# The sample tile's latents in float32 on four column groups, and an earlier page table load, in the first stage of a decode step

## The chip, the cores and the metric

The kernel runs on one core of one Trainium2 chip. The metric is the device time of one execution in microseconds; the time before is the median of three runs. The profile is of one further execution of the same program on the same kind of core.

## The reference, cut to what matters

One step of a hybrid decoder over 1024 prompt rows and 32 sample rows (8 sequences of 4 tokens). The part that the change touches is the norm of the input and the projection to the MLA latents:

```python
def rmsnorm(x, w):
    xf = x.astype(jnp.float32)
    xf = xf * lax.rsqrt(jnp.mean(xf * xf, axis=-1, keepdims=True) + EPS)
    return xf.astype(x.dtype) * w

z = rmsnorm(x, ln_w) @ w_in              # D_MODEL = 1024
rq, rk, rv, rg, cq, ckv, kr, mg, ga, gb = split(z)
q = rmsnorm(cq, q_norm_w) @ w_uq         # cq: 384 columns
ckv = rmsnorm(ckv, kv_norm_w)            # ckv: 256 columns
kr = rope(kr, pos)                       # kr: 64 columns
```

The 384 + 256 + 64 = 704 columns are called the latents. The sample rows then attend to a paged cache, for which `page_table` (8 x 64 numbers) is turned into a list of rows to gather. All results are float32, and the products are wanted at about that precision.

## The kernel before

The 1056 rows stand in nine tiles: tiles 0 to 7 are the prompt (128 rows each), tile 8 is the sample (32 rows). Most products are made in a split form: a float32 operand is parted into a rounded high part and a low remainder (both of type float32r), and `mac` (L261) adds three matmuls, high by high, high by low and low by high. The kernel is written in a framework that places the semaphores and lays out the order of each engine's instructions itself, by priority (the order of the source) and by its own estimate of when operands are ready. The order in a trace is therefore not line by line that of the source.

The first stage does this:

- `load_x(t)` (L300) loads a tile of x. `turn_tile(t)` (L342) squares and sums it on ACT (into a scratch tile `xs`, two buffers), makes the reciprocal root on POOL (`rstd_of`, L229), transposes the tile on PE in eight 128-column pieces (`turn_input`, L313), copies them out of PSUM and stores them to `xTD`.
- `scale_tile(t)` (L351) spreads the reciprocal root over the partitions with a small matmul (L355), multiplies on DVE (`y`, L358), and writes the high parts (`xh`, ACT, L363) and the low ones (`xl`, DVE, L364), eight of each. They stay in SBUF as `xn` for all later products of this input.
- `load_lat(k)` (L305) loads rows 128k to 128k+127 of the latents' weights into a raw tile `wlr` (four buffers for eight loads), makes the high part on ACT or POOL in turn, and the low part on DVE (`lo_of`, L198). A raw buffer is free again when both are made.
- `latent_tile(t)` (L386) makes the latents of a tile: 8 x 3 matmuls of 384 columns into one PSUM bank and 8 x 3 of 320 into another, with the tile's rows as the stationary operand; then the two norms (ACT L398, POOL, DVE L400), the rotation (`rope_nat`, L367) and the stores. For tile 8 the stationary operand has 32 columns, the number of matmuls is the same 48, and the result is kept in `latS`.
- `page_rows()` (L427) loads the page table, spread over all partitions, and turns it into the row numbers `idx` with four DVE instructions (L431 to L436). Its two tiles `pt_all` and `own` share the two `xs` buffers.

The tiles go in the order 0, 1, 8, 2, 3, 4, 5, 6, 7 (L444). Before the loop over them, tile 0 is turned and scaled, the weights are loaded, with x tiles 1 and 8 among them, and tile 1 is turned and scaled. In the loop `latents()` (L456), step n turns the tile two places on, makes the latents of its own tile, and scales the tile two places on. The page table follows in step 4. From step 6 the loop hands out time, and `beside` (L128) puts gate products (`gate_tiles`, L410) between: these load their weights into the two `wr` buffers of the pool `wst` and store their results through the two `gev` buffers of the same pool. All DMAs named here are issued by SP, whose queue is in order: an issue that waits for a buffer holds those behind it.

A later part, `sample_queries` (L503), already has products of the form that the change uses: four float32 matmuls with 32 stationary columns each, written to the four 32-partition groups of one PSUM bank (L527). L655 and L686 are of that kind too.

Of the kernel before, what the change touches and what calls it, by code (L numbers as in the profile page):

```python
# [161 lines left out]
def decode_step(ctx: ExitStack, tc: tile.TileContext, A: dict, O: dict):  # L162
# [20 lines left out]
    def ac():  # L183
        return banks["pool"].tile([P, 512], F32, tag="ac", name="ac", bufs=3)
# [119 lines left out]

    def load_lat(k):  # L305
        hi, lo = (p1.tile([P, NLAT], F32R, tag=f"wl{s}{k}", name=f"wl{s}{k}", bufs=1) for s in "hl")
        raw = p1.tile([P, NLAT], F32, tag="wlr", name="wlr", bufs=4)
        sp.dma_start(raw, w_in[k * P:(k + 1) * P, C_LAT:C_LAT + NLAT])
        (hi_pool if k % 2 else act.copy)(hi, raw)
        lo_of(lo, raw, hi)  # L310
        wlat.append((hi, lo))

    def turn_input(t, src, dst, nf, by=act.copy):  # L313

# [27 lines left out]
    def turn_tile(t):  # L342
        n = rows(t)
        xt = xts.pop(t)
        ss = small(p1, "ss")
        xs = p1.tile([P, D], F32, tag="xs", name="xs", bufs=2)
        act.activation(xs[:n], xt[:n], AF.Square, accum_out=ss[:n])
        r = rstd_of(p1, ss, n, 1.0 / D, dve if t == 0 else pool)
        turned[t] = r, turn_input(t, xt, xTD, D // P, dve.tensor_copy if t == 0 else act.copy)

    def scale_tile(t):  # L351
# [31 lines left out]
    latS = lp.tile([NR, NLAT], F32, name="latS")  # L383
    idx = lp.tile([P, NB * NPG // 16], I32, name="idx")

    def latent_tile(t):  # L386
        n = rows(t)
        pq, pk = ac(), ac()
        for ps, lo, w in ((pq, 0, QL), (pk, QL, KL + ROPE)):
            for k in range(8):  # L390
                xk = tuple(v[:, t * P:t * P + n] for v in xn[k])
                wk = tuple(v[:, lo:lo + w] for v in wlat[k])
                mac(ps[:n, :w], xk, wk, k == 0, k == 7)
        la = latS if t == 8 else p1.tile([P, NLAT], F32, tag="la", name="la", bufs=2)
        cq, kv, kr = la[:n, 0:QL], la[:n, QL:QL + KL], la[:n, QL + KL:NLAT].unsqueeze(1)
        for src, dst, w, nw in ((pq[:n, :QL], cq, QL, qnw), (pk[:n, :KL], kv, KL, kvw)):
            ss = small(p1, "ss2")
            act.activation(dst, src, AF.Square, accum_out=ss[:n])  # L398
            r = rstd_of(p1, ss, n, 1.0 / w)
            dve.scalar_tensor_tensor(out=dst, in0=src, scalar=r[:n], in1=nw[:n], op0=ALU.mult, op1=ALU.mult)  # L400
        rope_nat(kr, pk[:n, KL:KL + ROPE].unsqueeze(1), t, n, p1, 1, "kro")
        if t < 8:
            sp.dma_start(O["ckv_prompt"][0, 0, t * P:(t + 1) * P, :], kv)
            sp.dma_start(O["krope_prompt"][0, 0, t * P:(t + 1) * P, :], la[:, QL + KL:])
            turn_blocks(latD, p1.tile([P, NLAT], F32, tag="lt", name="lt", bufs=2), la, t, P)
        else:
            sp.dma_start(O["ckv_sample"].rearrange("l b t c -> (l b t) c"), kv)
            sp.dma_start(O["krope_sample"].rearrange("l b t c -> (l b t) c"), la[:n, QL + KL:])
# [16 lines left out]
                 gate_tiles(C_RG, [t[:, f, :] for t in gtD for f in range(4)], range(16), AF.Silu), gate_tiles(C_MG, mgD, range(4), AF.Silu))  # L425

    def page_rows():  # L427
        pt_all = p1.tile([P, NB * NPG], I32, tag="xs", name="pt_all", bufs=2)
        sp.dma_start(pt_all, A["page_table"].rearrange("b n -> (b n)").unsqueeze(0).to_broadcast([P, NB * NPG]))
        own = p1.tile([P, NB * NPG], F32, tag="xs", name="own", bufs=2)  # L430
        dve.tensor_copy(own, pt_all)  # L431
        own = own.rearrange("p (i g) -> p i g", g=16)
        dve.tensor_tensor(out=own, in0=own, in1=C("page").unsqueeze(1).to_broadcast([P, NB * NPG // 16, 16]), op=ALU.mult)
        row = small(p1, "row", NB * NPG // 16, 1)
        dve.tensor_reduce(out=row, in_=own, axis=AX.X, op=ALU.add)
        dve.tensor_scalar(idx, row, C("mod"), None, op0=ALU.add)  # L436

    head = at["maskT"][0]
    load_x(0)
    sp.dma_start(cst[:, :head], A["consts"][:, :head])  # L440
    sp.dma_start(lnw, A["ln_w"][0].rearrange("(f p) -> p f", p=P))
    turn_tile(0)
    scale_tile(0)
    order = [0, 1, 8, 2, 3, 4, 5, 6, 7]  # L444
    for k in range(8):
        load_lat(k)
        if k % 4 == 0:
            load_x(order[1 + k // 4])
    sp.dma_start(qnw, A["q_norm_w"][0:1, :].to_broadcast([P, QL]))
    sp.dma_start(kvw, A["kv_norm_w"][0:1, :].to_broadcast([P, KL]))  # L450
    sp.dma_start(ropeM, A["ropeM"])
# [2 lines left out]
    load_x(order[3])  # L454

    def latents():  # L456
        for n, t in enumerate(order):
            if n + 4 < 9:
                load_x(order[n + 4])
            if 0 < n < 7:  # L460
                turn_tile(order[n + 2])
            latent_tile(t)
            if n == 0:
                turn_tile(order[2])
            if n < 7:
                scale_tile(order[n + 2])
            if n == 1:
                sp.dma_start(cst[:, head:], A["consts"][:, head:at["turn"][0]])
                sp.dma_start(gnw, A["ret_gn_w"][0].rearrange("(f p) -> p f", p=P))
            if n == 4:  # L470
                page_rows()
            yield 7.1 if n > 5 else 0.0

    beside(latents(), 3 * 7.1, fill, 36)
# [1141 lines left out]
```

## Time and profile before

| | before |
|---|---|
| median of 3 runs | 2159.27 us (2158.21 to 2162.92) |
| the profiled execution | 2150.59 us |
| its span, first to last instruction | 2148.7 us |
| mean granted TensorE clock | 0.996 |
| ACT, POOL busy | 723.7, 326.4 us |
| HBM read, written | 236.96, 68.36 MB |

Times in the views are microseconds from the span's start. PE is TensorE's matmul side, PEld its weight load, DVE the vector engine, ACT the scalar engine, POOL GpSimd, SP the engine that issues the DMAs. A line of the timeline has the start, the length, the engine, the line of the kernel, the operation, the tiles written and read, and in brackets how long the engine stood idle before it and what ended that. A matmul's length includes its way through the array, and the next one begins before it ends; what a matmul holds PE for is the distance from its start to the next start. A float32 matmul (as against float32r) leaves two records.

### The profile page before, as it was taken

The numbers are of one execution on the slowest core, as the hardware profiler recorded it, in microseconds if no ns is written. First come the engines' busy times: TensorE is split into PE (matmuls) and PEld (weight loads), VectorE is DVE, ScalarE is ACT, GpSimd is POOL, SyncE is SP. The second block draws the span as 40 slices with busy tenths as digits, with TensorE's granted clock in tenths as the row PEclk, the third lists the DMA queues.
The fourth block names the chain that finished last, engine by engine and source line by source line (L and its number), as shares of the span: only waits on it lengthen the run. The fifth ranks groups of instructions, "written<-read, shape, count | busy, mean of one in ns | idle before, by whom it ended". The sixth has DMA issues, their size and how long they took to land.

```text
span 2148.7 us, 38490 instructions
## 1 busy us (share of the span) xinstructions
PE 2107.3 (98%) x15192; PEld 1841.5 (86%) x15192; DVE 1261.0 (59%) x2832; ACT 723.7 (34%) x1514; POOL 326.4 (15%) x519
## 2 busy tenths in 40 slices
PE   8999999999999999999999999999999999999998
PEld 7898787777777998888888887788888999999998
DVE  5534556565565357676676764877776353444465
ACT  5412222342433322222222312454555341322343
POOL 2210111111110022222222220122211000000122
PEclk9999999999999999999999999999999999999999
DMA  7476656566564422644634637210112453324243
GB/s 209 124 221 232 233 194 234 212 231 237 200 231 165 124 65 72 206 115 121 197 75 147 179 87 259 58 45 18 38 51 80 151 176 95 100 80 127 79 144 118
DMA packets 325876, 307.83 MB, mean 143 GB/s; under 512 B 91648, under 2 KB 283264, under 8 KB 321600
## 3 DMA queue, kind: packets, MB, share of 16 engines
q1 hardware_dynamic: 316480, 221.50, 34.6%
q0 software_dynamic: 9216, 83.89, 10.5%
q8 instruction: 119, 1.95, 0.4%
q14 instruction: 61, 0.50, 0.1%
HBM read 236.96 MB, written 68.36 MB: 142 GB/s over the span
## 4 chain that ended last, share of the span: by engine, by line
PE 87%; DVE 2%; ACT 1%; DMA 1%; issue 1%; POOL 1%; SPq 0%; ACTq 0%; DVEq 0%; POOLq 0%
PE mm L265 22%; PE mm L266 20%; PE mm L267 20%; PE sc L655 4%; PE x L686 3%; PE ac L267 2%; PE ac L265 2%; PE ac L266 2%; PE mm L1313 2%; PE tr L1299 1%; PE tr L865 1%; PE ac L1038 1%; PE ac L1256 1%; PE x L680 1%; PE ac L887 1%
## 5 line engine op out<-in xcount | busy, mean ns | idle before, releaser
L265 PE MATMUL mm<-xh,wh 128*128 128x352 f32 x1344 | 455.2, 339 | 0.2
L267 PE MATMUL mm<-xh,wl 128*128 128x352 f32 x1344 | 434.3, 324 | 2.1 <-DVE wl L199 2.1
L266 PE MATMUL mm<-xl,wh 128*128 128x352 f32 x1344 | 434.9, 324 | 0.0
L265 PEld LDWEIGHTS mm<-xh,wh 128*128 128x128 f32 x1344 | 252.2, 188 | 90.5 <-issue 76.5
L266 PEld LDWEIGHTS mm<-xl,wh 128*128 128x128 f32 x1344 | 253.3, 188 | 3.3 <-issue 1.0
L267 PEld LDWEIGHTS mm<-xh,wl 128*128 128x128 f32 x1344 | 253.0, 188 | 3.3 <-DVE wl L199 2.6
L199 DVE TENSOR_TENSOR wl<-wr,wh 128x512 fp32r<-128x512 f32 (+2 forms) x251 | 173.8, 704 | 120.4 <-ACT wh L246 101.8
L246 ACT CAST wh<-wr 128x512 fp32r<-128x512 f32 x216 | 129.8, 618 | 294.9 <-PE mm L266 221.0
L651 DVE STREAM_TRANSPOSE kt<-craw 128x512 f32<-128x512 f32 x256 | 160.7, 681 | 84.8 <-PE sc L655 79.7
L416 ACT ACTIVATE gev<-mm 128x352 f32<-128x352 f32 x120 | 55.6, 464 | 237.2 <-PE mm L267 157.0
L267 PE MATMUL mm<-gh,wl 128*128 128x352 f32 x384 | 124.3, 324 | 0.0
L267 PE MATMUL mm<-mh,wl 128*128 128x352 f32 x384 | 124.3, 324 | 0.0
L265 PE MATMUL mm<-mh,wh 128*128 128x352 f32 x384 | 124.3, 324 | 0.0
L265 PE MATMUL mm<-gh,wh 128*128 128x352 f32 x384 | 124.3, 324 | 0.0
L266 PE MATMUL mm<-ml,wh 128*128 128x352 f32 x384 | 124.2, 324 | 0.0
L266 PE MATMUL mm<-gl,wh 128*128 128x352 f32 x384 | 124.2, 323 | 0.0
L265 PE MATMUL mm<-wv,xh 128*128 128x512 f32 x256 | 103.7, 405 | 0.0
L266 PE MATMUL mm<-wv,xh 128*128 128x512 f32 x256 | 100.9, 394 | 0.0
L267 PE MATMUL mm<-wv,xl 128*128 128x512 f32 x256 | 100.7, 394 | 0.0
L655 PE MATMUL sc<-kt,q 32*32 32x512 f32 x2560 | 91.2, 600 | 0.0
L854 ACT ACTIVATE on<-ac,gb,gs 128x512 f32<-128x512 f32 (+1 forms) x36 | 28.0, 778 | 179.6 <-DVE gb L852 179.6
L1546 POOL TENSOR_TENSOR xr<-x1h,x1l 128x352 f32<-128x352 f32 x24 | 27.1, 1154 | 389.9 <-DVE pT L199 311.9
(382 smaller groups left out, 4540.0 us busy)
## 6 DMA issues: line engine op xcount, KB each, us to landing
wr<-in_w_in_dram SPq DMA_DIRECT2D x144, 256.0 KB, 3.1
st<-in_state_ret_dram SPq DMA_DIRECT2D x32, 512.0 KB, 4.5
out_ret_sample_dram<-st SPq DMA_DIRECT2D x32, 512.0 KB, 3.8
wr<-in_w_ple_gate_dram SPq DMA_DIRECT2D x48, 256.0 KB, 2.9
gt<-gev SPq DMA_DIRECT2D x48, 176.0 KB, 3.9
gl<-go SPq DMA_DIRECT2D x16, 528.0 KB, 5.8
gate<-ga SPq DMA_DIRECT2D x16, 528.0 KB, 3.5
g<-gt SPq DMA_DIRECT2D x32, 256.0 KB, 3.2
```

Of the source, the lines that this page charges most:

```text
L199: dve.tensor_tensor(out=out, in0=src, in1=b32(hi), op=ALU.subtract)
L246: hi_by[0](hi, raw)
L265: pe.matmul(out, wh, xh, start=first, stop=False)
L266: pe.matmul(out, wh, xl, start=False, stop=False)
L267: pe.matmul(out, wl, xh, start=False, stop=last)
L416: act.activation(t, ps, func)
L651: dve.transpose(kt[:, 2 * i + s].rearrange("p (n r) -> p n r", r=32), src)
L655: pe.matmul(sc[32 * v:32 * v + 32, q, :], Q["q4"][qs_, j + v // 2, 2 * (g % 2) + v % 2, :], kt[qs_, v, :], start=n == 0, stop=n == NJ // 2 ...
L686: pe.matmul(pv[32 * v:32 * v + 32, :KL], pT[:, n, 32 * v:32 * v + 32], keys[v % 2][:, 8 * (v // 2) + n, :], start=n == 0, stop=n == 7, til ...
L854: act.activation(on[:n], po, AF.Identity, bias=nb[:n], scale=s[:n])
L1313: pe.matmul(po[:, :256], v[a][w], t[:, x, 256 * a:256 * a + 256], start=j + a + part == 0, stop=False, skip_group_check=True)
L1546: pool.tensor_tensor(out=xr, in0=b32(x1[f][0][:, sl]), in1=b32(x1[f][1][:, sl]), op=ALU.add)
```

## The change

- The sample tile's latents are no longer made by 48 split matmuls in step 2, but inside `latent_tile(0)`: behind the three matmuls of each of the eight weight pieces, four float32 matmuls use the raw piece as it is, each with the 32 sample rows as stationary operand, 176 of the 704 columns, and one of the four partition groups of a bank (`sample_latents`).
- Their operand `xS` is the turned sample tile times the norm's weight `ln_w`, made on POOL. The reciprocal root of the rows is not in it; it is copied to `r8` and multiplied in at the end, on DVE, after ACT has moved the four groups out of PSUM (in `latent_tile(8)`).
- For this, x of tile 8 is loaded first after tile 0 and the constants, and tile 8 is turned before the weights 1 to 7 are loaded. Its scaling to `xn` (wanted by later products) stays where it was. x of tile 1 is loaded behind the first weights.
- The raw weights get five buffers instead of four; a buffer is now held until the sample's matmuls have read it.
- `page_rows` becomes a generator in two halves: the load in step 2, the DVE part in step 4. `pt_all` and `own` move from the `xs` buffers to the `wr` buffers; `xS` uses a `gev` buffer; the PSUM bank is one of the two `mm` banks.

```diff
     def load_lat(k):
         hi, lo = (p1.tile([P, NLAT], F32R, tag=f"wl{s}{k}", name=f"wl{s}{k}", bufs=1) for s in "hl")
-        raw = p1.tile([P, NLAT], F32, tag="wlr", name="wlr", bufs=4)
+        raw = p1.tile([P, NLAT], F32, tag="wlr", name="wlr", bufs=5)
         sp.dma_start(raw, w_in[k * P:(k + 1) * P, C_LAT:C_LAT + NLAT])
         (hi_pool if k % 2 else act.copy)(hi, raw)
         lo_of(lo, raw, hi)
-        wlat.append((hi, lo))
+        wlat.append((hi, lo, raw))
...
         r = rstd_of(p1, ss, n, 1.0 / D, dve if t == 0 else pool)
+        if t == 8:
+            r8 = small(p1, "r8", 1, 1)
+            pool.tensor_copy(r8[:n], r[:n])
+            r = r8
...
+    NG = NLAT // 4
+
+    def sample_latents(k):
+        for r in range(4):
+            pe.matmul(few[0][r * NR:(r + 1) * NR, :NG], few[1][:, k], wlat[k][2][:, r * NG:(r + 1) * NG], start=k == 0, stop=k == 7,
+                      tile_position=(0, r * NR), skip_group_check=True)
+
     def latent_tile(t):
         n = rows(t)
-        pq, pk = ac(), ac()
-        for ps, lo, w in ((pq, 0, QL), (pk, QL, KL + ROPE)):
-            for k in range(8):
-                xk = tuple(v[:, t * P:t * P + n] for v in xn[k])
-                wk = tuple(v[:, lo:lo + w] for v in wlat[k])
-                mac(ps[:n, :w], xk, wk, k == 0, k == 7)
+        if t < 8:
+            pq, pk = ac(), ac()
+            for ps, lo, w in ((pq, 0, QL), (pk, QL, KL + ROPE)):
+                for k in range(8):
+                    xk = tuple(v[:, t * P:t * P + n] for v in xn[k])
+                    wk = tuple(v[:, lo:lo + w] for v in wlat[k][:2])
+                    mac(ps[:n, :w], xk, wk, k == 0, k == 7)
+                    if t == 0 and lo == 0:
+                        sample_latents(k)
+        else:
+            raw = p1.tile([NR, NLAT], F32, tag="la", name="las", bufs=2)
+            for r in range(4):
+                act.activation(raw[:, r * NG:(r + 1) * NG], few[0][r * NR:(r + 1) * NR, :NG], AF.Copy)
+            dve.tensor_scalar(raw, raw, few[2][:NR], None, op0=ALU.mult)
+            pq, pk = raw[:, :QL], raw[:, QL:]
...
     def page_rows():
-        pt_all = p1.tile([P, NB * NPG], I32, tag="xs", name="pt_all", bufs=2)
+        pt_all = wst.tile([P, NB * NPG], I32, tag="wr", name="pt_all", bufs=2)
         sp.dma_start(pt_all, A["page_table"].rearrange("b n -> (b n)").unsqueeze(0).to_broadcast([P, NB * NPG]))
-        own = p1.tile([P, NB * NPG], F32, tag="xs", name="own", bufs=2)
+        yield
+        own = wst.tile([P, NB * NPG], F32, tag="wr", name="own", bufs=2)
         dve.tensor_copy(own, pt_all)
...
     sp.dma_start(lnw, A["ln_w"][0].rearrange("(f p) -> p f", p=P))
+    load_x(8)
     turn_tile(0)
     scale_tile(0)
     order = [0, 1, 8, 2, 3, 4, 5, 6, 7]
-    for k in range(8):
+    load_lat(0)
+    load_x(1)
+    turn_tile(8)
+    few = [mm(), wst.tile([P, 8, NR], F32, tag="gev", name="xS", bufs=2), turned[8][0]]
+    for half, st in enumerate(turned[8][1]):
+        fs = slice(4 * half, 4 * half + 4)
+        pool.tensor_tensor(out=few[1][:, fs], in0=st[:, :, :NR], in1=lnw[:, fs].unsqueeze(2).to_broadcast([P, 4, NR]), op=ALU.mult)
+    for k in range(1, 8):
         load_lat(k)
-        if k % 4 == 0:
-            load_x(order[1 + k // 4])
...
     def latents():
+        table = page_rows()
         for n, t in enumerate(order):
             if n + 4 < 9:
                 load_x(order[n + 4])
             if 0 < n < 7:
                 turn_tile(order[n + 2])
             latent_tile(t)
-            if n == 0:
-                turn_tile(order[2])
             if n < 7:
                 scale_tile(order[n + 2])
...
-            if n == 4:
-                page_rows()
+            if n in (2, 4):
+                next(table)
             yield 7.1 if n > 5 else 0.0
```

More of the change, by code (lines that the diff above doesn't have):

```diff
@@ L436, in page_rows @@
         dve.tensor_scalar(idx, row, C("mod"), None, op0=ALU.add)
+        yield
     head = at["maskT"][0]
```

## The prediction

> **What bounds the kernel now.** I read the page's head first, then PE's busy time stage by stage (the windows view; columns: stretch, its length, busy us of PE, weight load, DVE, ACT, POOL, granted clock, DMA share, GB/s), then the list of what PE waited for.
>
> ```profile
> span 2148.7 us, 38490 instructions
> PE 2107.3 (98%) x15192; PEld 1841.5 (86%) x15192; DVE 1261.0 (59%) x2832; ACT 723.7 (34%) x1514; POOL 326.4 (15%) x519
> ```
> ```profile
> 0.00:20.00 20.00, 12.40 (x61) 11.12 (x61) 12.58 (x25) 11.76 (x25) 5.70 (x11) 1.00 0.84 244
> ```
> ```profile
> 28.00:36.00 8.00, 8.00 (x47) 7.96 (x47) 3.78 (x17) 6.02 (x18) 1.49 (x4) 0.79 0.73 149
> ```
> ```profile
> 45.00:75.00 30.00, 30.00 (x193) 29.59 (x191) 17.78 (x58) 15.59 (x46) 5.04 (x14) 1.00 0.83 195
> 150.00:2149.00 1999.00, 1972.28 (x14372) 1712.92 (x14371) 1187.98 (x2629) 664.36 (x1352) 291.55 (x441) 1.00 0.44 141
> ```
> ```profile
> PE ac L1256 <- ACT pr L1274: 7.4, 6, 3.1
> PE tr L355 <- POOL rs_r L234: 7.1, 4, 3.3
> ```
>
> The reader is to see that PE is the bound nearly everywhere: a microsecond of matmul taken out of the 28 to 75 us stretch, where PE has no gap, moves the end unless another engine is late there. The second largest wait, 7.1 us at L355, lies wholly in the first stage, which the change rewrites. Only DMA and the start-up chain bound the first 12.7 us.
>
> **What it removes.** The sample tile's latents are 48 matmuls (three groups, each like the first row below, of 8 + 8), back to back on a full PE (the timeline: start, length, engine, line):
>
> ```profile
> L265 PE MATMUL ac<-wlh,xh x144: 307/334/667, 12.7 to 127.6; 128*128 128x384 f32 x64, 128*128 128x320 f32 x64, 128*32 128x384 f32 x8, 128*32 128x320 f32 x8
> ```
> ```profile
> 36.31 0.42 PE L265 MATMUL ac<-wlh,xh 128*32 128x384 f32 x1
> ...
> 43.94 0.31 PE L267 MATMUL ac<-wlh,xl 128*32 128x320 f32 x1
> 44.09 0.38 PE L355 MATMUL tr<-cst,rs_r 128*128 128x128 f32 x2
> ...
> 52.92 0.38 PE L355 MATMUL tr<-cst,rs_r 128*128 128x128 f32 x2
> ```
> From 36.31 to 44.09: **7.78 us** gone (0.162 a product). The full tile behind it takes from 44.09 to 52.92, 8.83 us.
>
> Next, a wait that tile 8 causes by being turned late:
>
> ```profile
> 24.91 0.19 POOL L232 TENSOR_SCALAR rs_v<-ss 128x1 f32<-128x1 f32 x1 [4.58 <-ACT la L398]
> ```
> ```profile
> 27.46 0.40 PE L355 MATMUL tr<-cst,rs_r 32*128 32x32 f32 x2 [1.91 <-POOL rs_r L234]
> ```
> POOL took tile 0's norm (waiting for ACT L398) before tile 8's, so PE stood **1.91 us** at tile 8's scale. With tile 8 turned before the weights its rstd is long there. Behind that gap the clock fell: 0.79 over 28 to 36 us is 8 x 0.21 = **1.70 us** lost. I count it as going with the gap. The Trainium skill ("TensorE: Matmul & The Clock Gate", section "HAM oscillation — how this bites in real kernels") puts the danger at idle gaps over about 3.4 us; by that rule a 1.91 us gap would not be the cause and the sum would lack 1.70. The trace speaks against it: the clock fell behind 1.91 us, and not behind the 3.28 us below.
>
> Tile 8's eight transposes leave the busy stretch for the idle start (start to next start 0.61):
>
> ```profile
> 19.33 0.68 PE L322 MATMUL tr<-cst,xt 32*128 32x32 f32 x8
> 19.94 0.44 PE L267 MATMUL ac<-wlh,xl 128*128 128x384 f32 x1
> ```
> **0.6 us**; PE had 7.6 of the first 20 us free.
>
> Last, the page table:
>
> ```profile
> 72.40 0.43 DVE L431 CAST own<-pt_all 128x512 f32<-128x512 int32 x1 [3.75 <-DMA pt_all<-in_page_table_dram]
> 73.59 0.69 DVE L435 TENSOR_REDUCE row<-own 128x32 f32<-128x512 f32 x1
> 75.67 1.05 ACT L347 ACTIVATE xs<-xt 128x1024 f32<-128x1024 f32 x1
> 76.83 1.06 ACT L347 ACTIVATE xs<-xt 128x1024 f32<-128x1024 f32 x1
> 78.31 0.49 PE L355 MATMUL tr<-cst,rs_r 128*128 128x128 f32 x2 [3.28 <-POOL rs_r L234]
> ```
> pt_all and own sit in the two xs slots, so the squares of tiles 6 and 7 (L347, into xs) cannot run before the reduce ends at 74.28; they then queue behind L398 on ACT, POOL's power follows, and PE waits **3.28 us**. After the change both tables live in wr, nobody waits for xs, and the table has landed two tiles earlier. The wr slots are next wanted by the gates' first weights; DVE needs 1.8 us of cast, product and reduce, now without a DMA wait, so they come free before PE wants those weights. Removed in all: 7.78 + 1.91 + 1.70 + 0.60 + 3.28 = **15.27 us**.
>
> **What it adds.** Eight rounds of four float32 matmuls, 32 stationary columns, 176 moving; float32 leaves two records each, so 64. The trace has two column-tiled kin:
>
> ```profile
> 217.78 0.32 PE L267 MATMUL mm<-xh,wl 128*128 128x352 f32 x1
> 218.03 3.66 PE L686 MATMUL x<-craw,pT 128*32 128x256 f32 x64
> 221.62 0.43 PE L265 MATMUL mm<-xh,wh 128*128 128x352 f32 x1
> ```
> ```profile
> 150.47 0.32 PE L266 MATMUL mm<-xl,wh 128*128 128x352 f32 x1
> 150.73 0.83 PE L527 MATMUL mm<-early 128*32 128x384 f32 x2
> 151.49 0.43 PE L267 MATMUL mm<-xh,wl 128*128 128x352 f32 x1
> 151.76 0.32 PE L265 MATMUL mm<-xh,wh 128*128 128x352 f32 x1
> ```
> L686 is the same pattern, 8 rounds of 8 records at 256 columns: 3.59 us from start to next start, 0.449 a round, 1.75 ns a column. 176 columns: 0.31 a round, 2.5 for eight. Breaking the stream costs extra: the lone matmul at 150.73 holds PE from 150.63 (a normal start 0.16 after 150.47) to 151.49, and the next takes 0.27 for 0.16: 0.97, against 384 x 1.75 ns = 0.67, so 0.30 a break. One block costs 2.8, eight separate rounds 8 x 0.61 = 4.9. Each stands between tile 0's products, and the first two fall before the clock is up, so I take **5.2** (bounds 2.8 and 7.8, no saving over the old form). The Trainium skill ("TensorEngine Tiling (Array Packing)", "Key Properties") speaks against mixing: a change of tiling mode drains the array. It gives no price; by its rule the rounds' number decides, which is the gap between my 2.8 and 4.9.
>
> The start. Tile 8's 128 KB now go ahead of the first weights: 0.54 us at the 244 GB/s above. Its square (1.04 us at 32 rows) and two copies go on ACT, its norm, the copy r8 and two products of 128 columns on POOL (nearest row 1.15 us at 352 columns, so under that each; from nothing up to 2.3). ACT has a 2.04 us wait for the first weights there, and POOL nothing before the second weights:
>
> ```profile
> 7.64 0.78 ACT L309 CAST wlh<-wlr 128x704 fp32r<-128x704 f32 x1 [2.04 <-DMA wlr<-in_w_in_dram]
> ```
> ```profile
> L1546 POOL TENSOR_TENSOR xr<-x1h,x1l 128x352 f32<-128x352 f32 x24 | 27.1, 1154 | 389.9 <-DVE pT L199 311.9
> ```
> ```profile
> 16.31 1.04 ACT L347 ACTIVATE xs<-xt 32x1024 f32<-32x1024 f32 x1
> ```
> ```profile
> 11.57 4.63 SPq L308 DMA_DIRECT2D wlr<-in_w_in_dram  x3
> ```
> SP also gets tile 8's two xTD stores ahead of weights 1 to 7, and weights 5 to 7 now wait for PE's rounds 0 to 2 as well as DVE (the 4.63 us is SP standing for those buffers). Behind them stand the norms' weights, the rope table and later x tiles. PE has tile 1's products to fill with, so I take **0.8** for the first matmul alone (bounds -0.3, if tile 8's square fits into ACT's wait and the first product no longer stands behind tile 1's scale, and 2.5, if ACT's 1.04 + 2 copies and the later weights add up).
>
> What is late next: the lead. Tile 2 is scaled after tile 1's products, and the sample tile's 7.78 us covered that:
>
> ```profile
> 35.30 0.38 PE L355 MATMUL tr<-cst,rs_r 128*128 128x128 f32 x2
> 35.52 1.04 PE L322 MATMUL tr<-cst,xt 128*128 128x128 f32 x8
> ```
> ```profile
> 36.68 2.45 ACT L363 ACTIVATE xh<-y,lnw 128x128 fp32r<-128x128 f32 x8
> ```
> ```profile
> 40.06 1.09 DVE L364 SCALAR_TENSOR_TENSOR xl<-y,lnw,xh 128x128 fp32r<-128x128 f32 x4
> ```
> ```profile
> 40.82 0.48 ACT L398 ACTIVATE latS<-ac 32x384 f32<-32x384 f32 x1 [1.22 <-PE ac L267]
> ```
> The eight xh take 2.45 us from 36.68, so the first is there at 37.0, 1.7 us behind the start of L355; the transposes of tile 3 (35.52 to 36.31) cover 0.8 of that, so PE idles 0.9. The last xl ends at 41.15; PE, 21 products of 0.162 on from 37.0, wants it at 40.4: 0.75 more. The sample's evacuation (four ACT copies of 176 columns, each below the 0.48 of 384; one DVE scaling; then its norm and rope as before) now stands on ACT and DVE ahead of tile 3's scaling with no products of its own over it; 0.55 is my choice for that. In all **2.2**. The low bound is 0: if tile 2's scale is planned a little earlier, the products of tile 1 cover it. The high bound is one tile's whole DVE work uncovered: 17.78 us in 30 is 59%, of 8.83 us **5.2**.
>
> **The sum.** -15.27 + 5.2 + 0.8 + 2.2 = **-7.1 us**. The profiled execution took 2150.59 (span 2148.7 and 1.9 around it), so 2143.5 by its own time. The median shown is 8.7 above that execution; I take the difference over: 2159.27 - 7.1 = **2152.2**.
>
> **The rivals.**
> Forecast, 2147.5 to 2155: 0.54.
> (1) The planner merges rounds and scales tile 2 early: 2.4 and 2.2 more, 2147.6. For: each engine's order is laid out by a planner and not as the source has it (tile 8's transposes stand inside the products of tiles 0 and 1), and it fills PE's gaps with what it holds ready. Against: rounds become ready one weight at a time. 0.12.
> (2) DVE binds behind tile 1 and the weights come late: 5.2 for 2.2, 2.5 for 0.8, and one fall of the clock, 1.7: 2152.2 + 6.4 = 2158.6; half of that, 2155.4, already counts here. For: DVE is 63% busy in 0 to 20. Against: its 59% in 45 to 75 leaves room. 0.16.
> (3) The page table does less than it says: the 3.28 us come from ACT's order (L398 ahead of both squares), which stays: 2155.5. Against: the two squares stand together, right behind the reduce. 0.08.
> (4) Slower. The planner's order after 150 us falls out differently, with the waits of L1256 on ACT as the place. PE idles 1999 - 1972.28 = 26.7 us there; half as much again is 13.4, and 2152.2 + 13.4 = 2165.6. It decides from 7.1 us of new idle. For: those waits hang on which product stands where. Against: nothing in that stage is edited. 0.10.
>
> A measurement here tells about 0.2%, 4.3 us, from no change. Faster: 0.54 + 0.12 = 0.66; same (2155 to 2163.6): 0.24; slower 0.10. The range, 2146.5 to 2159.5, takes in (1) to (3) and leaves out (4) and the tails.
>
> **What would show it.** Right: no 128*32 products with 384 columns behind tile 1; L355 waits under 2 us in sum; no 3 us gap near 70; the float32 records taking 0.3 to 0.6 a round; tile 2's products starting some 4 us sooner. Wrong: rounds over 0.8 us, the first product after 15 us, a PE wait on xh or xl over 4 us, the half clock lasting beyond 18 us, or PE's idle time after 150 us growing by more than 5.

## The result: no gain, 0.2% slower

| | before | after | ratio, 95% interval |
|---|---|---|---|
| first comparison, median of 12 runs each | 2160.15 us | 2164.02 us | 1.0018 (1.0010 to 1.0026) |
| second comparison, another chip (23 and 11 runs) | 2151.61 us | 2155.56 us | 1.0020 (1.0011 to 1.0029) |
| profiled execution, first of each | 2150.59 us | 2163.64 us | |

Forecast were 2152.2 us, in 2146.5 to 2159.5, against the first pair: 11.8 us too low. One thing has to be known before the traces are compared: chips differ by 9 us for one and the same kernel (medians of before: 2151.6 and 2152.4 on two of them, 2160.6 and 2160.7 on two others; the place is shown under `b0`). By its time and that place, the first profile of before is of the first kind, that of after of the second. So the changed kernel's profile `a1_again` (2154.69 us), of the first kind, is compared with before's, and the changed kernel's first profile with `b0`, before once more on the second kind. One of the eleven runs of `s1` below took 4106.44 us and is left out of its ratio.

The page of the changed kernel, first profile (instructions and busy time), has 16 matmul records more than before's 15192 and PE is busy 1.4 us less than the 2114.4 of `b0`:

```profile
span 2161.8 us, 38520 instructions
...
PE 2113.0 (98%) x15208; PEld 1842.6 (85%) x15208; DVE 1259.5 (58%) x2833; ACT 722.7 (33%) x1518; POOL 326.2 (15%) x522
```

What PE waited for from 0 to 165 us (engine, tile, line, releaser: total us, times, longest), first a row of before, then `a1_again`:

```profile
PE mm L267 <- DVE wl L199: 2.1, 2, 1.5
```
```profile
PE tr L322 <- DMA cst<-in_consts_dram: 6.3, 1, 6.3
PE tr L359 <- POOL rs_r L234: 2.5, 3, 1.2
PE mm L265 <- ACT gev L436: 2.3, 1, 2.3
PE mm L265 <- POOL wh L196: 2.1, 1, 2.1
PE mm L267 <- DVE wl L199: 2.1, 1, 2.1
PE ac L265 <- DVE la L420: 1.8, 1, 1.8
```

The 3.28 us wait for `rs_r` has gone (longest now 1.2). The last four rows make 8.3 us, of which before had only the one for `wl` (2.1 us): gate products (`mm`) that wait for their weights and for a bank to be emptied, and a latent product for its bank. The cause of the first ones is on SP's queue (timeline, the gates' first weights `wr`): before, then `a1_again`.

```profile
70.19 1.45 SPq L245 DMA_DIRECT2D wr<-in_w_in_dram  x2
```
```profile
86.94 2.05 SPq L332 DMA_DIRECT2D latD<-lt  x4
89.03 1.15 SPq L245 DMA_DIRECT2D wr<-in_w_in_dram  x2
```

They are issued 19 us later, behind the stores of a later tile. In before, gate products fill the gaps of the last latent tiles from 83 us on; now the first one starts at 98.06 us, and the clock falls twice, where the first profile of before has one fall in this stage (windows view of `a1_again`; after the first three numbers come busy times, then the granted clock, the DMA share and GB/s):

```profile
84.10:87.50 3.40, 3.40 (x14) 3.40 (x14) 3.31 (x13) 0.10 (x2) 1.08 (x2) 0.50 0.16 48
...
101.10:104.50 3.40, 3.40 (x14) 3.40 (x13) 0.48 (x2) 0.00 (x0) 0.82 (x2) 0.51 0.81 196
```

From some 163 us on all engines run the same instructions in the same order as before (the last 14293 records of PE and 2615 of DVE agree one by one). The time of one DVE instruction, counted from the end of the program, can therefore be compared stage by stage. The table has the difference to the reference profile in us, computed so from the records:

```
kernel (profile)             to 163   163-729  729-1352  rest   span
first kind of chip, against before's first profile
changed, a1_again             -0.08    +0.79    +3.26   +0.21   +4.2
p1  before, 16 records more   -0.38    +0.95    +4.36   +1.05   +6.0
p2  changed, 112 more         -2.90    +0.73    +1.02   +1.61   +0.5
g3  changed, three groups     -3.64    +0.99    +1.53   +0.25   -0.8
s1g3 sample alone, three gr.  -3.55    +1.12    +1.84   -0.61   -1.2
f3  changed, weights early    +3.26    +1.01    +2.64   +0.13   +7.1
d2  before, 24 fewer          -5.26    -0.03    +2.99   -0.24   -2.5
d1  before, 48 more           +8.09    +3.72    +7.89   +0.10  +19.8
second kind, against b0       to 162   162-735  735-1360
changed, first profile        -2.09    -0.92    +5.75   +0.92   +3.6
changed, a0                   -3.51    -0.41    +1.31   +0.07   -2.6
t1  table alone               -1.23    +0.31    +0.20   +0.70   -0.1
s1  sample alone              -4.35    +0.01    +4.69   +1.39   +1.7
s1p sample alone, 112 more    -2.10    -0.47    +0.34   -0.00   -2.3
p3  before, 128 more          +2.29    -0.22    +0.84   +0.89   +3.8
p4  before, 64 more           +4.78    -0.39    +7.62   +0.19  +12.2
```

A single profile carries 3.4 us windows of half clock, 1.7 us each, that come or not; so its rows tell where, and the medians how much. Two rows flatter: before has such a window at 1343 us and so have `a1_again` and `p1` at 1347 and 1348, but `p2` and `g3` have none between 729 and 1352 us. If it cost them its 1.7 us there too, their 1.02 and 1.53 would be some 2.7 and 3.2, near the 3.26 of `a1_again`.

### The profile page after: what moved, and what is told of

Read it like the earlier page. It is cut to its first block, busy times and chain, and to the rows that moved or that the text cites. A ratio compares the mean times of both kernels' runs of the same rounds, so it can differ in the third digit from the quotient of the medians.

```text
span 2161.8 us, 38520 instructions
## 1 busy us (share of the span) xinstructions
PE 2113.0 (98%) x15208; PEld 1842.6 (85%) x15208; DVE 1259.5 (58%) x2833; ACT 722.7 (33%) x1518; POOL 326.2 (15%) x522
## 3 DMA queue, kind: packets, MB, share of 16 engines
q8 instruction: 119, 1.95, 0.4%
## 4 chain that ended last, share of the span: by engine, by line
PE 64%; DVE 3%; DMA 1%; issue 1%; ACT 1%; POOL 1%; SPq 0%; ACTq 0%; DVEq 0%; POOLq 0%
PE mm L265 16%; PE mm L266 15%; PE mm L267 15%; PE ac L267 2%; PE ac L266 2%; PE ac L265 2%; PE mm L1340 2%; PE tr L1326 1%; PE sc L682 1%; PE ac L1283 1%; PE x L713 1%; PE ac L1065 1%; PE tr L892 1%; PE ac L1285 1%; PE ac L1284 1%
## 5 line engine op out<-in xcount | busy, mean ns | idle before, releaser
L265 PE MATMUL mm<-xh,wh 128*128 128x352 f32 x1344 | 457.1, 340 | 4.1 <-POOL wh L196 2.1
L265 PEld LDWEIGHTS mm<-xh,wh 128*128 128x128 f32 x1344 | 253.7, 189 | 94.8 <-issue 77.2
L678 DVE STREAM_TRANSPOSE kt<-craw 128x512 f32<-128x512 f32 x256 | 160.7, 680 | 108.1 <-PE sc L682 73.5
L265 PE MATMUL mm<-mh,wh 128*128 128x352 f32 x384 | 124.3, 324 | 0.0
L265 PE MATMUL mm<-gh,wh 128*128 128x352 f32 x384 | 124.3, 324 | 0.0
L265 PE MATMUL mm<-wv,xh 128*128 128x512 f32 x256 | 103.8, 405 | 0.0
L1573 POOL TENSOR_TENSOR xr<-x1h,x1l 128x352 f32<-128x352 f32 x24 | 26.5, 1128 | 389.9 <-DVE pT L199 313.5
```

The costliest lines, as they stand in the source:

```text
L265: pe.matmul(out, wh, xh, start=first, stop=False)
L678: dve.transpose(kt[:, 2 * i + s].rearrange("p (n r) -> p n r", r=32), src)
L1573: pool.tensor_tensor(out=xr, in0=b32(x1[f][0][:, sl]), in1=b32(x1[f][1][:, sl]), op=ALU.add)
```

## The experiments

### Is it the execution? `b0` and `a0`

Both kernels unchanged, one run each.

> The kernel before again, unchanged, for a second profile. In the first profile of before (2150.6 us, some 9.5 us under the median of its runs) all 16 second score groups of the sample attention release ScalarE 0.19 to 0.42 us after their last product; in the profile of after 12 of 16 do so only 1.7 to 2.5 us after it, in an instruction order that is the same on every engine from about 170 us on. Theory 1 (an execution draws it, whatever the kernel): this profile shows late releases (about 2 us) in some of the 16 groups too, and a span of 2156 to 2160. Theory 2 (the change brings them): none of the 16 is later than 0.5 us and the span is near 2149.

> The changed kernel again, unchanged, for a second profile. Theory 1 (drawn by the execution): the number of late releases differs from the 12 of the first profile, and the span moves with it, by about 0.5 us for each. Theory 2 (brought by the change): about 12 again, span near 2162. In both the end of tile 5's latents lies some 9 us ahead of before (74 us), and the first gate weights are issued only at about 88 us.

`b0` took 2160.02 us, `a0` 2157.39. In `b0` before shows the late releases too, in 13 of 16 groups (13, not 12, also in the changed kernel's first profile), and so do all profiles on this kind of chip, the same groups in each. Theory 1 holds so far that the change does not bring them; but the execution does not draw them either: they go with the chip. (Each chip served one comparison, so something else that differs between the comparisons isn't ruled out.) The timeline of before, first profile, and of `b0` (score products, then ACT's copy of the sums):

```profile
302.23 1.14 PE L655 MATMUL sc<-kt,q 32*32 32x512 f32 x32
...
303.56 1.01 ACT L666 COPY sums<-sc 64x1024 f32<-64x1024 f32 x1 [1.19 <-PE sc L655]
```
```profile
301.17 1.14 PE L655 MATMUL sc<-kt,q 32*32 32x512 f32 x32
...
304.35 1.01 ACT L666 COPY sums<-sc 64x1024 f32<-64x1024 f32 x1 [3.05 <-remote]
```

The same two instructions stand 1.33 us apart in the one and 3.18 in the other. From 163 to 729 us that made `b0` 9.6 us longer. It is no part of the change, and it is where the 8.7 us came from that separated before's profile from its median.

### The two halves alone: `t1_table_alone`, `s1_sample_alone`

```diff
# t1: before, with the changed page_rows() in wr and
-            if n == 4:
-                page_rows()
+            if n in (2, 4):
+                next(table)
# s1: the changed kernel, with page_rows() in xs and
-            if n in (2, 4):
-                next(table)
+            if n == 4:
+                page_rows()
```

> Before with only the page table's part of the change: load two tiles ahead, both tiles in the raw gate weights' buffers. In the order made for SyncE the gates' first weights then stand at place 64 instead of 56, behind later tiles' stores, as in the changed kernel. Theory A (that place is what gives the first stage's gain back): the 3.28 us wait at 75 us goes, but the gates' first weights are issued after 85 us instead of at 70, and gates no longer fill the gaps of the last tiles: slower than before by 2 to 6 us (2162 to 2166). Theory B (the place costs nothing; the loss comes from the sample's part): faster by about 3 us (2157).

> The changed kernel with the page table's part taken back: tables in the squares' buffers, loaded and used in step 4; the gates' first weights stand at place 56 again. Theory A: the sample's part keeps its gain, without the 3.28 us of the table: sum 7.78 + 1.91 + 1.70 + 0.60 less 5.2 and 0.8, about 6 us faster than before (2154), and the gates' weights are issued near 62 to 70 us. Theory B (the sample's part gives back what it gains): within 2 us of before (2158 to 2162).

Each gave 0.9999 of before (0.9990 to 1.0008 and 0.9989 to 1.0008). The table alone is ahead by 1.23 us at 162 us: the 3.28 us wait went, and waits for `wh`, `wl` and `gev` (2.1 + 2.1 + 0.7 us) came, with the weights issued at 86.31 us. So theory A named the place, but not the price: at the end gain and price cannot be told apart from nothing. The sample alone is ahead by 4.35 us there, its weights issued at 66.98 us, and loses 4.7 us between 735 and 1360 us, in an order that is the same as before's. Neither theory had that loss.

### Where the later loss comes from: `a1_again`, `f3_weights_early`, `d1_sample_twice`, `d2_sample_half`

```diff
# f3: the changed kernel, the first gate weights loaded in step 4
+            if n == 4:
+                ready.append(load_w(w_in[:, C_GA:C_GA + P], 8))
...
-            w = load_w(w_in[:, col + f * P:col + (f + 1) * P], 8)
+            w = ready.pop() if ready else load_w(w_in[:, col + f * P:col + (f + 1) * P], 8)
# d1: before
-            for k in range(8):
+            for i in range(16 if t == 8 else 8):
+                k = i % 8
# d2: before
-            for k in range(8):
+            for k in range(4 if t == 8 else 8):
```

> The changed kernel unchanged, timed beside the others on one chip. The table alone and the sample alone came out at 0.9999 of before each. Theory A (each part gains 3 to 4 us by 160 us, and the two together no more than one, since both parts' order issues the gates' weights late): by 160 us 3.5 to 4 us ahead of the second profile of before, 1 us of it lost at 735 to 890 us, and the time at 0.999 to 1.000. Theory B (the two parts disturb each other in a way that neither shows alone, as the first comparison's 1.0018 says): 1.001 to 1.0026 again.

> The changed kernel with the load of the gates' first weight tile put into step 4, behind the table's DVE part; SyncE then issues it at place 56, not 64. Theory A (the late gate weights gave back the gain): the waits of the gate products for their weights (2.1 + 2.1 us in the second profile of the changed kernel) and the wait behind tile 7's copies go, gate products run between the last tiles, and the lead at 160 us is about 3 us more than in the changed kernel, 6.5 to 7 us: 0.9985 to 0.999 of the changed kernel. Theory B (the weights' place is not the cause, the ACT order is): the lead stays at 3.5 to 4 us and the time with it.

> Before with the 48 products of the sample tile's latents made twice (the second pass is the one kept): 7.8 us more of back-to-back products on a full TensorE. Theory A (what is taken out of or put into this stretch moves the end by its length): 2160.6 + 7.8 = 2168.4, 1.0036. Theory C (later stages hold slack, by a transfer or another engine that sets their starts, and take up a part of it): under 1.0025, with the offset shrinking between 735 and 1400 us.

> Before with only four of the eight weight pieces in the sample tile's latents (24 products of 48; half of that sum is left out): 3.9 us less. Theory A: 0.9982. Theory C (the lead is taken up later, as 1 us at 735 to 890 and some 2 us up to 1360 in the profiles of the changed kernel and of the sample alone): 0.999 to 1.000, the offset at 160 us near -3.9 and at the end near -1.

`a1_again`: 1.0020, theory B's number, and at 163 us level with before, not 3.5 us ahead: its constants landed 1.5 us later (6.3 us for 4.8) and one more window of half clock fell into this stage. `f3`: 1.0049 (1.0037 to 1.0061), worse, so bringing the loads forward in this way does not help. The weights came at 65.58 us; gate products then ran in front of the last tile's latents, and POOL, whose order has the last tile's norm ahead of the second weights, stood still (timeline of `f3`, POOL):

```profile
99.29 0.19 POOL L232 TENSOR_SCALAR rs_v<-ss 128x1 f32<-128x1 f32 x1 [11.52 <-ACT la L418]
...
106.28 0.19 POOL L232 TENSOR_SCALAR rs_v<-ss 128x1 f32<-128x1 f32 x1 [6.16 <-ACT la L418]
...
107.07 1.20 POOL L196 TENSOR_SCALAR wh<-wr 128x512 fp32r<-128x512 f32 x2
```

The wait went from the first weights to the second (the row of L265 for `wh` has 4.3 us, 2 times). Four windows of half clock fell into this stage (80.8, 108.1, 111.5 and 138.9 us), two more than in `a1_again`; at 1.7 us each that is 3.4 us. `f3` is 3.3 us behind it at 163 us, though its constants landed 1.4 us sooner. `d2`, which leaves out half of the sample's sum, 24 products, was 5.3 us ahead at 163 us and ended at 0.9996 (0.9987 to 1.0004). `d1`, 48 products more, 7.8 us of work, was 8.1 us behind at 163 us and ended at 1.0074 (1.0061 to 1.0087), 16 us. So theory A of a plain shift falls, and C too: `d2` alone would fit it, but slack would take up a delay as it takes up a lead, and in `d1` the delay doubled. What `s1`, `d1`, `d2`, `f3` and the changed kernel have in common, and `t1` lacks, is another number of matmuls ahead of the rest.

One jump was the same in all profiles with 16 records more: a gate product at 882 to 890 us waits for its weights. Before, then `a1_again` (timeline, SP and ACT; the DMA view of the 4 us from 877.4, with queue and packets):

```profile
877.43 0.97 SPq L245 DMA_DIRECT2D wr<-in_w_in_dram  x2
...
880.93 0.62 ACT L246 CAST wh<-wr 128x512 fp32r<-128x512 f32 x1 [0.21 <-DMA wr<-in_w_in_dram]
```
```profile
q1 hardware_dynamic: 1049, 0.71, 63.8%
...
wr<-in_w_in_dram SPq DMA_DIRECT2D x2, 256.0 KB, 2.8
```
```profile
878.09 0.97 SPq L245 DMA_DIRECT2D wr<-in_w_in_dram  x2
...
882.63 0.62 ACT L246 CAST wh<-wr 128x512 fp32r<-128x512 f32 x1 [1.16 <-DMA wr<-in_w_in_dram]
```
```profile
q1 hardware_dynamic: 1176, 0.77, 71.7%
q8 instruction: 1, 0.02, 1.5%
...
wr<-in_w_in_dram SPq DMA_DIRECT2D x2, 256.0 KB, 3.3
```

Issue to use is 3.50 us in before and 4.54 in the changed kernel, and there a packet of queue q8 lies in between. The page of before lists that queue, kind "instruction", with 119 packets and 1.95 MB:

```profile
q8 instruction: 119, 1.95, 0.4%
```

That is 16 KB a packet, busy for about 1 us, one every 18 us on average. PE's 15192 matmul and 15192 weight-load records over 119 packets make 128 of each a packet, 64 bytes apiece; and the profiles with 48, 64 or 128 matmul records more than before have 120 packets. So a packet's place in the program goes by the count of matmuls ahead of it. By the count alone 16 records more would move it by an eighth of the distance, some 2.4 us. At this place it moved further: it starts 1.92 us behind the issue in `a1_again` and 7.19 us in before, and 7354 PE records before the end for 7327. Why 27 records and not 16 stays open.

What the packet does to the load can be read from the load's own packets. The line of the timeline (x2) is two loads of 256 KB. The first lands 2.64 us behind that issue in before and 2.73 in `a1_again`; the second, 512 packets of 512 bytes, is told as landed after 3.48 and 4.51 us, though half of its packets are there after 2.58 and 2.56. This is the DMA view from 3.22 us behind the issue on, when in before all packets are there; before (880.65 to 881.4 us), then `a1_again` (881.31 to 882.2):

```profile
DMA packets 0, 0.00 MB, mean 0 GB/s; under 512 B 0, under 2 KB 0, under 8 KB 0
```
```profile
q1 hardware_dynamic: 26, 0.01, 7.3%
```

In `a1_again` 25 of the load's packets (and one small one) are still to come. They land one after another, the last 4.08 us behind the issue (3.18 in before), and hold 7.3% of 16 engines, about one engine. Spread evenly, 512 packets would be 32 an engine. So what is late is about one engine's share of the load, behind the instruction packet, which ran from 1.92 to 2.85 us, and the whole load waits for it.

### The count alone: `p1_before_16_more`, `p2_after_128_more`, `g3_three_groups`, `s1g3_sample_alone_three`

```diff
# p1: before, 8 tiny products; p2: the changed kernel, 56
+    nil = small(p1, "nil", 32, 1)
+    pool.memset(nil, 0.0)
+    idle = [mm(), mm()]
+    for i in range(8):
+        pe.matmul(idle[0][:32, :32], nil, nil, start=True, stop=True)
     load_x(0)
# g3 (changed kernel) and s1g3 (s1)
-    NG = NLAT // 4
+    G3 = ((0, 256), (256, 256), (512, 192))
...
-        for r in range(4):
-            pe.matmul(few[0][r * NR:(r + 1) * NR, :NG], few[1][:, k], wlat[k][2][:, r * NG:(r + 1) * NG], ...
+        for r, (at_, m) in enumerate(G3):
+            pe.matmul(few[0][r * NR:(r + 1) * NR, :m], few[1][:, k], wlat[k][2][:, at_:at_ + m], ...
```

> Before with 8 tiny float32 products (32 x 32, 16 matmul records, result unused) at the very start, where TensorE stands idle for 5 to 6 us until the constants land. No work is added where TensorE is busy; what changes is that the program has 16 matmul records more ahead of everything, as the changed kernel has. TensorE's instructions are fetched in packets of 16 KB, about one for every 128 matmul records; in all kernels with 16 records more (changed kernel, sample alone) such a packet starts 1.9 to 2.2 us after the gate weights' load issued at 878 to 882 us, and those weights are used 4.5 to 4.8 us after their issue; in before it starts 7 us after, and they are used after 3.5 us. Theory F (the fetch stands in the way of waited-for loads, and its place in the program moves with the count of matmuls): 4.5 us or more from that issue to the use, 735 to 890 us longer by 0.9 to 1.1 us, and the whole at 1.0010 to 1.0020 of before. Rival (chance, or something else of the change): 3.5 us there, 1.000.

> The changed kernel with 56 such tiny products (112 records) at the start, so that it has 128 records more than before, a whole packet, and the fetches fall where they fall in before. Theory F: 735 to 890 us as in before (its 0.9 to 1.1 us gone), 735 to 1360 us shorter than in the changed kernel by 3 to 4 us; the time 0.9985 to 0.999 of the changed kernel's, that is 1.000 to 1.001 of before, plus what the tiny products delay the start if the idle time there doesn't hold them (up to 3 us, seen in the first 20 us). Rival: as the changed kernel, 1.002.

> The changed kernel with three column groups of 256, 256 and 192 columns in place of four of 176: 48 matmul records in place of 64, as many as the split form had, so that the program has before's count again. Each round is longer by 80 columns x 1.75 ns = 0.14 us, 1.1 us for eight. Theory F: the later loss of 3 to 4 us goes, 0.9985 to 0.9995 of the changed kernel and 1.000 to 1.001 of before. Rival: 1.002 to 1.0025 of before.

> The sample's part alone (page table as before) with three column groups: before's count of matmul records, and the gates' first weights at place 56. Theory F: ahead by 4.35 - 1.1 = 3.2 us at 162 us, and kept to the end: 0.9985 of before, faster than both kernels. Rival (every lead is taken up later, whatever the count): 0.9995 to 1.0005.

`p1` adds sixteen records that take 1.06 us in PE's idle start. The planner lays out the first 65 us a little differently (83 of PE's 330 records there have changed places); from 65 us on PE's order is before's (timeline of `p1`, PE):

```profile
0.92 1.06 PE L443 MATMUL mm<-nil 128*32 128x32 f32 x16 [0.92 <-POOL nil L440]
4.72 1.94 PE L322 MATMUL tr<-cst,xt 128*128 128x128 f32 x8 [2.74 <-DMA cst<-in_consts_dram]
```

It is 0.4 us ahead at 163 us and ends at **1.0035** of before (1.0022 to 1.0049), some 6 us later by the medians. At the known place the packet is there again (timeline and DMA view of `p1`), with 4.77 us from issue to use:

```profile
877.85 0.97 SPq L245 DMA_DIRECT2D wr<-in_w_in_dram  x2
...
882.62 0.62 ACT L246 CAST wh<-wr 128x512 fp32r<-128x512 f32 x1 [1.35 <-DMA wr<-in_w_in_dram]
```
```profile
q8 instruction: 1, 0.02, 1.4%
...
wr<-in_w_in_dram SPq DMA_DIRECT2D x2, 256.0 KB, 3.5
```

The first part of the forecast came true: 729 to 900 us is 1.0 us longer. With the count made up to before's or to a whole packet more, the loss is gone from the time of the whole, in all three: `p2` 0.9999 (0.9990 to 1.0008), `g3` 0.9997 (0.9988 to 1.0006), `s1g3` **0.9984** (0.9975 to 0.9993), faster than both kernels. Their packets come 6.3 to 7.0 us behind that issue, as in before (7.2), and the weights are used 3.5 to 3.6 us behind it; from 870 to 900 us they are level with before (0.0, 0.0 and 0.1 us), where `a1_again` loses 1.0 and `p1` 1.3. For the rest of the stage the traces do not show a gain: `p2` was to be 3 to 4 us shorter there than the changed kernel and is 2.2, of which the missing window of half clock can be 1.7. The size I gave was too small: the 16 records cost 0.35%, not 0.10 to 0.20. In `g3` and `s1g3` the rounds cost more than the 1.1 us I had said, since PE's order breaks the stream 11 times instead of 9 (they hold PE for 7.1 us in `g3` and 4.8 in the changed kernel); what is left of the lead at 163 us is 3.6 us in both.

### Place or count: `p3_before_128_more`, `p4_before_64_more`, `s1p_sample_alone_112_more`

The same edit with 64, 32 and 56 tiny products. Still open was whether `p2` gained by its warm start.

> Before with 64 tiny products (128 records, one whole packet of instructions) at the start. Theory F: the fetches fall where they fall in before (about 7 us behind the issue of the gate weights at 877 us, use 3.5 us behind it), and 735 to 1360 us is within 0.5 us of before's; what is left is what the products do to the start, where they run in idle time and raise the clock (a gain of up to 1 us): 0.9993 to 1.0003. Rival (any products at the start cost something, as 16 records cost 1.0035): 1.0035 or more.

> Before with 32 tiny products (64 records, half a packet): the fetches move by half their distance, some 10 us earlier in the program than in before, so none falls between issue and use of the gate weights at 877 us (use 3.5 us behind the issue), but others fall elsewhere. Theory F: a time that neither before nor the 16 records give, 0.998 to 1.003 by where the fetches fall; the 735 to 890 us stretch as in before. Rival (the count itself costs): between 1.0035 and the time with 128 records.

> The sample's part alone, four column groups, with 112 tiny records at the start, so that the program has 128 more than before. Theory F: the sample alone, 0.9999 before with its 16 records more, keeps its 4.35 us to the end: 0.998 of before, 0.0004 under the three groups by their shorter rounds. Rival (three groups are better for another reason): 0.9999 as the sample alone.

A whole packet more leaves before as it was: `p3` 1.0001 (0.9992 to 1.0010), though it runs eight times the tiny products of `p1`, and has PE's order of `p1` from 65 us on. Half a packet gives `p4` 1.0034 (1.0022 to 1.0047), with the 882 us place untouched (3.59 us). In its profile 7.6 us are lost elsewhere in 735 to 1360 us, and 4.8 us before that, where it has four windows of half clock and `b0` one. `p3`, with more tiny products, has 2.3 us there, so a part of `p4`'s loss may come from the start. `p1` and `p3` show it without that: the place of the fetches matters, and not the number of records by itself. `s1p` took 0.9988 (0.9979 to 0.9997), where 0.998 was expected: the sample's part alone gains once its count is made up, with four groups as with three.

In all 17 profiles at hand the 882 us place sorts the same way: packet 1.9 to 2.2 us behind the issue, 4.54 to 4.80 us to the use (six profiles); packet 6.3 us or more behind, or 6.2 ahead, 3.40 to 3.62 (ten). One, `d1`, has it 3.2 us ahead and 4.20. A second place is the load of the retention state at 1310 to 1325 us, for which PE waits up to 1.9 us in `a1_again` and `p1` and 0.5 in before; `g3` and `s1g3` still wait 1.6 and 1.3 us there, so the count doesn't explain that place. The 882 us place is shown, then, and is worth 1.0 to 1.3 us. By the medians `p1` is 6.1 us behind before; where the rest of that arises is not shown.

## Why the prediction was wrong

**What it had right.** The sample's part of the sum, in part by luck. It forecast -7.78 - 1.91 - 1.70 - 0.60 + 5.2 + 0.8 + 2.2 = -3.8 us; `s1` was 4.35 us ahead at 162 us and `s1g3` 3.55 at 163. By its terms, in the first profile of the changed kernel (timeline, PE):

```profile
20.23 0.34 PE L265 MATMUL ac<-wlh,xh 128*128 128x384 f32 x1
20.50 0.80 PE L394 MATMUL mm<-wlr,xS 128*32 128x176 f32 x14
21.22 0.41 PE L265 MATMUL ac<-wlh,xh 128*128 128x320 f32 x1
...
22.24 0.49 PE L394 MATMUL mm<-wlr,xS 128*32 128x176 f32 x2
22.66 0.44 PE L266 MATMUL ac<-wll,xh 128*128 128x384 f32 x1
...
38.73 0.49 PE L359 MATMUL tr<-cst,rs_r 128*128 128x128 f32 x2 [1.16 <-POOL rs_r L234]
38.98 0.42 PE L265 MATMUL ac<-wlh,xh 128*128 128x384 f32 x1
```

The rounds hold PE for 4.8 us in nine pieces (a piece of eight records 0.44, of two still 0.42, of fourteen 0.73), plus 0.1 us each on the product ahead and the one behind: 6.4 us in all, 5.6 without the first piece, which fell into the idle start. So 5.2 was a little low, and the price of a break right (0.42 and 0.2, less 0.31, for 0.30). In `b0` tile 2's products start at 42.78 us (timeline, PE):

```profile
42.78 0.42 PE L265 MATMUL ac<-wlh,xh 128*128 128x384 f32 x1
```

In the changed kernel they start 3.80 us before that; forecast were some 4. The lost lead shows as 1.16 us in front of tile 2's scale, not as waits for xh and xl, and is within the 2.2. The start was mis-sized: the first product came at 11.97 us, 0.55 sooner than the 12.52 of `b0`, where I had 0.8 later. The luck is that the 1.70 us of clock in this sum never came (below), and that the start and the lead together were better than forecast by some 2.4 us.

**What failed, first: "they come free before PE wants those weights".** That sentence gave the page table its 3.28 us. The buffers do come free early (first profile of the changed kernel, timeline, DVE: the last read of `own`), but that is not what sets the weights' time.

```profile
68.37 0.68 DVE L456 TENSOR_REDUCE row<-own 128x32 f32<-128x512 f32 x1
```

The planner had put the gates' first weights beside the table's stall, as the 68th issue of SP that the trace counts; with the table early they are the 82nd, behind the stores of later tiles (places 56 and 64 in the planner's list). The trace lacked none of this: the row at 70.19 us was there, and I had not asked what made it come then. The table's part is worth 1.2 us by itself at 162 us, and 0.9999 (0.9990 to 1.0008) at the end (`t1`). On top of the sample's part it is worth less than nothing: at 162 us `a0`, with both, is 3.51 us ahead, and `s1`, without it, 4.35. In the changed kernel the four waits of 8.3 us stand against 3.28 and 1.91 us gone and 2.1 us of `wl` that was there before.

**The 1.70 us of clock** (8 x 0.21 is 1.68; a window of 3.41 us at half clock is 1.7) did not belong to the gap. In `b0`, the same kernel as before, the same wait of 1.90 us at 27.61 us leaves the clock up, and the clock falls at 77.5 us, right behind the 3.28 us wait (timeline, PE; windows view of `b0`):

```profile
27.61 0.40 PE L355 MATMUL tr<-cst,rs_r 32*128 32x32 f32 x2 [1.90 <-POOL rs_r L234]
```
```profile
76.85 0.49 PE L355 MATMUL tr<-cst,rs_r 128*128 128x128 f32 x2 [3.28 <-POOL rs_r L234]
```
```profile
29.00:32.40 3.40, 3.40 (x27) 3.39 (x26) 2.03 (x9) 3.40 (x11) 0.74 (x2) 1.00 0.64 110
77.50:80.90 3.40, 3.40 (x16) 3.40 (x15) 3.40 (x12) 1.83 (x6) 3.02 (x7) 0.50 0.30 91
```

So one profile of before could not tell which wait the half clock follows: in the first it was the short one, in `b0`, `p1`, `s1` and `s1g3` the 3.28 us one. In `a1_again` it fell at 84 and 101 us, behind waits of 1.79 us and of 2.13 and 2.10 us. The rule of the Trainium skill that I weighed there ("TensorE: Matmul & The Clock Gate", "HAM oscillation — how this bites in real kernels"), which asks for no idle gaps over about 3.4 us, does not cover those: no wait between 80 and 105 us in that profile is longer than 2.13 us.

**What failed, second: the step from the sum to the end.** "a microsecond of matmul taken out of the 28 to 75 us stretch [...] moves the end unless another engine is late there" left out that the change alters the number of matmuls, and with it the place of every later instruction fetch. By the ratios above that costs 0.35% in `p1` against before, and the changed kernel is 0.23% above `g3` (1.0020 and 0.9997, on two chips). In `a1_again` 3.3 us are lost between 729 and 1352 us; 1.0 of them is shown to be a fetch, at the 882 us place. Nothing in the sum stood for it.

**Rival (4)** came nearest in number, 2165.6 against 2164.0, by luck, since its mechanism is another: the order after 163 us is the same row for row, and the waits of L1256 did not grow by more than 0.3 us in that stage (4.1 us in before, 4.4 at L1283 in `a1_again`, 729 to 1410 us). One sign that I had named for being wrong did show: PE's idle time after 150 us grew by 5.0 us, from 26.5 to 31.5 in `a1_again`. Rival (3), that the 3.28 us stay, is refuted: they went.

**The base.** I carried an 8.7 us difference between the profiled execution and the median over as a constant. It was one, but of the chip: the runs and the profiled execution were on chips of different kinds.

## What to carry to other kernels

Moving a load or a stall also moves what the planner had built around it: before counting a stall as gained, look up what the order had placed in it, and what is issued next on each queue. In a kernel that is PE-bound with loads landing just in time, compare variants at the same count of matmuls modulo one instruction packet (here 128), or shift each by a few idle products before judging it; otherwise up to 0.35% of the difference is the place of the fetches and not the edit. The part that was worth keeping is the sample's alone with the count made up: 0.9984 of before.

## What the runs showed of the hardware

- Instruction fetches show as queue q8, 119 or 120 packets of 16 KB. One that starts 1.92 us behind the issue of the gate weights' load in `a1_again` holds up about one engine's share of it: the last packet lands at 4.08 us and not at 3.18. Sixteen matmul records in idle time cost 1.0035 (1.0022 to 1.0049); 128 cost 1.0001 (0.9992 to 1.0010).
- The same program releases ACT and DVE 0.2 us after the last 32x32 score product on some chips (two of those compared) and 2.0 us after it on others (two), in the same 13 of 16 groups, worth 9.6 us between 163 and 729 us. The cause stays open.
- Windows of half clock start at multiples of 3.41 us from each other: in `a1_again` at 84.1, 101.1, 1347.0 and 1384.6 us, 5, 365 and 11 such steps apart. Which wait they follow differs between executions of one kernel: 1.91 us in the first profile of before, 3.28 us in `b0`.
